# Start addresses of the feed-forward weight forms in a hybrid decoder block

## The chip, the core and the metric

The kernel runs on one core of one Trainium2 chip. The metric is the device time of one execution in microseconds (us), as the median of the runs shown. The profile below is one more execution, taken by the hardware profiler.

## What is computed

The reference is one decoder layer over 512 positions with 1024 channels, in float32. First comes a mixer of two branches (a gated short convolution, and a sparse attention with compressed, selected and windowed keys), merged by gates and projected by `w_o`. The change concerns the second half alone, the feed-forward part:

```python
h = rmsnorm(x, norm2_g[l])
gu = h @ w_ffn_in[l]                       # 1024 -> 2 * 2816
g = causal_dwconv(gu[..., :D_FF], ffn_conv_w[l]) + ffn_conv_b[l]
x = x + (jax.nn.silu(g) * gu[..., D_FF:]) @ w_ffn_out[l]
```

## The kernel before

Every dense product is made of three passes of TensorE in a 4-byte format: both operands are split into a high part and a low part (`split`, lines 151 to 154: ScalarE copies the value to the high part, VectorE subtracts), and hi times hi, hi times lo and lo times hi are added up in PSUM (`dense`, lines 400 to 406: for each k the two products with the high weights, lines 403 and 404, and after them all products with the low weights, line 406). In this document a weight tile is the stationary operand that TensorE loads (LDWEIGHTS), 128 x 128 values at a time, 512 bytes in each partition; the activation is the moving operand that streams past it.

**The feed-forward stage.** It works on two tiles of 128 output channels at a time (`ff_strassen`, line 954): 11 pairs of tiles, each once for the gate half (n = 0) and once for the up half (n = 1) of `w_ffn_in`, 22 form sets in all. Each set is a 2 x 2 x 2 product by Strassen's scheme: seven products of 512 contraction rows (4 k) by 256 positions, so 7 x 4 x 3 = 84 matmuls of 128 x 256, 1848 in the whole stage. The activation forms `xf_h` and `xf_l` (lines 795 and 796) are made once and stay: 4 x 7 slices of 256 values, 1024 bytes each. The weight forms are made for each set by `ff_forms` (line 860):

- `a22`, half a weight tile, split into `th` and `tl` (tags `th` and `tl`, two buffers each, lines 871 and 872). The low part is made by ScalarE (minus the value) and a DMA from POOL's queue that adds the weight from memory (`dma_split`, line 156).
- `a11` and `a12`, a whole weight tile, split in the same way into `wh_s` and `wl_s`, buffers of the ring that the down projection also uses (`ring`, line 162).
- Two pairs of sums of the four blocks, forms 2 and 3 and forms 4 and 1, built by VectorE in `sf` buffers and split by ScalarE and VectorE into `sh` and `sl` (`put`, lines 880 to 885, 44 calls; tags `sh` and `sl`, three buffers each, NSQ = 3).

`ff_pair` (line 904) multiplies: first `a22` (`th`, `tl`), then `a11` and `a12` (`wh_s`, `wl_s`), then forms 2, 3, 4 and 1 (`sh`, `sl`). ScalarE copies the first finished product out of PSUM into `p1` (line 941), and VectorE's `sums` (line 919) adds it to the next bank. Between the two sets of a pair, `down_part` (line 975) does a part of the down projection with matmuls of 128 x 512 (`pdn`; moving `ah`/`al`, weights `wh_d`/`wl_d`). The framework's scheduler orders the instructions on each engine by a timeline of its own and puts in the waits.

**Where buffers start.** A pool hands out its buffers one behind the other, in the order in which the tags first appear, so a tile that is made only to claim a place (a `const` by the name of `gap`, or a first tile with a name that ends in `_`) moves what comes behind it. The pool `pw` (line 797) is such a row. What matters below is the start of a buffer behind a multiple of 512 bytes, here called its **place**. A weight slice is 512 bytes and a slice of `xf` 1024, so the place is the same for all k and all forms of a buffer. In this program the places are:

| buffers | place (bytes) | distance from `xf` |
|---|---|---|
| `xf_h`, `xf_l` | 288 | 0 |
| `th`, `tl` (two each) | 288 | 0 |
| `sh`, `sl` (three each) | 480 | 192 |
| `wh_s`, `wl_s`, `wh_d`, `wl_d` | 480 | 192 |
| `ah`, `al` (moving in the down projection) | 480 | 192 |

In the parts of the program ahead of the feed-forward stage nearly every moving and stationary tile is at place 480, so their distance is 0. The scores of the attention (lines 596 and 597) are the exception: the keys `kHH` and `kL` have rows of 544 values, and the distance between the queries (weights) and the keys (moving) is 0, 128, 256 or 384 by group, branch and first column.

Of the kernel before, what the change touches and what calls it, by code (L numbers as in the profile page):

```python
# [11 lines left out]
F32 = mybir.dt.float32  # L12
F32R = mybir.dt.float32r
# [5 lines left out]
P = 128  # L19
D = 1024  # L20
# [35 lines left out]
NSQ = 3  # L56
# [26 lines left out]
def tile_block(ctx: ExitStack, tc: tile.TileContext, xT, pos, par, par2, w_tok, w_a3, w_gate, w_ao, w_bo, w_o,  # L83
# [11 lines left out]
    def const(shape, name, dt=F32, pool=sb):  # L95
        return pool.tile(shape, dt, name=name, tag=name)

    def w_tmp(name, shape):

        t = pp.tile([P, TOKC], F32, name=name, tag="w4", bufs=NW4)  # L100
        v = t[:, :math.prod(shape)]
        if len(shape) == 2:
            v = v.rearrange("p (a b) -> p a b", a=shape[0])
        elif len(shape) == 3:
            v = v.rearrange("p (a b c) -> p a b c", a=shape[0], b=shape[1])
        return v
# [7 lines left out]
    def s_bank(name):  # L114
        return bank("s", name, 3)

    def t_bank(name):
        return bank("t", name, 2)

    def o_bank(name):  # L120
        return bank("o", name, 1)
# [29 lines left out]
    def split(h, l, v):  # L151
        hi = nc.scalar.activation(h, v, AF.Copy)  # L152
        nc.vector.tensor_sub(l, v, h.bitcast(F32))  # L153
        return hi

    def dma_split(h, l, raw, src, dst=None):

        nc.scalar.activation(h, raw, AF.Copy)  # L158
        nc.scalar.activation(l, raw, AF.Copy, scale=-1.0)  # L159
        nc.gpsimd.dma_start(l if dst is None else dst, src, accum_op=ALU.add)  # L160

    def ring(name):
        return (wf.tile([P, D], F32R, name=f"wh_{name}", tag="wh", bufs=NWF),
                wf.tile([P, D], F32R, name=f"wl_{name}", tag="wl", bufs=NWF))

    def raw_tile(name):
        return wf.tile([P, D], F32, name=f"wr_{name}", tag="wr", bufs=NRAW)
# [202 lines left out]
    def row_scales(total, name, bank_of, dg):  # L370

        pr = bank_of(f"pr_{name}")
        for t in range(NT):
            for i, v in enumerate(total):
                sums = nc.tensor.matmul(pr[:, 2 * t:2 * t + 2], v[:, t * P:(t + 1) * P], ones[:, 0:2],
                                        start=i == 0, stop=i == len(total) - 1)
        ms = sb.tile([P, NT], F32, name=f"ms_{name}", tag="ms")
        nc.vector.tensor_scalar(ms, pr[:, 0:2 * NT].rearrange("p (t two) -> p t two", two=2)[:, :, 0], 1.0 / D, EPS,
                                op0=ALU.mult, op1=ALU.add)
        means[name] = ms  # L380
        r = sb.tile([P, NT], F32, name=f"r_{name}", tag=f"r_{name}")
        rsqrt(r, ms, NT)
        nc.vector.tensor_tensor(dg, ident[:, None, :].to_broadcast([P, NT, P]), r[:, :, None].to_broadcast([P, NT, P]),
                                op=ALU.mult)
        for t in range(NT):
            rows = nc.tensor.matmul(pr[:, t * P:(t + 1) * P], ones, dg[:, t, :], start=True, stop=True)
        rb = sb.tile([P, S], F32, name=f"rb_{name}", tag="rb")
        nc.scalar.activation(rb, pr, AF.Copy)
        return r, rb, (sums, rows)

    r1, r1b, _ = row_scales((sq_sum[0][:, 0],), "n1", d_bank, w_tmp("dg_n1", (NT, P)))
# [8 lines left out]
    def dense(acc, units, first=True, last=True):  # L400

        for i, (wh, wl, xh, xl) in enumerate(units):
            nc.tensor.matmul(acc, wh, xh, start=first and i == 0, stop=False)  # L403
            nc.tensor.matmul(acc, wh, xl, start=False, stop=False)  # L404
        for i, (wh, wl, xh, xl) in enumerate(units):
            nc.tensor.matmul(acc, wl, xh, start=False, stop=last and i == len(units) - 1)  # L406
# [381 lines left out]
    TH = S // 2  # L788
# [6 lines left out]
    xf_h = const([P, 4, 7, TH], "xf_h", F32R, px)  # L795
    xf_l = const([P, 4, 7, TH], "xf_l", F32R, px)
    pw = ctx.enter_context(tc.tile_pool(name="pw", bufs=1, side="left"))
    for i in "hl":
        pw.tile([P, D // 2], F32R, name=f"t{i}_", tag=f"t{i}", bufs=2)
    const([P, 48], "gap_w", F32, pw)  # L800

    def x_forms(k, v):
        nc.vector.tensor_sub(v[:, T1:T3 + 1], v[:, 1:4:2], v[:, 0:2])
# [56 lines left out]
    def ff_forms(f, n):  # L860

        nm = f"{n}_{f}"
        raws = []
        for m in range(2):
            raw = raw_tile(f"s{nm}{m}")
            nc.sync.dma_start(raw, w_ff[f + m, n])
            raws.append(raw)
        a11, a12 = raws[0][:, 0:HALF_D], raws[0][:, HALF_D:]
        a21, a22 = raws[1][:, 0:HALF_D], raws[1][:, HALF_D:]
        form = {}  # L870
        h = pw.tile([P, HALF_D], F32R, name=f"th{nm}", tag="th", bufs=2)
        l = pw.tile([P, HALF_D], F32R, name=f"tl{nm}", tag="tl", bufs=2)
        dma_split(h, l, a22, w_ff[f + 1, n][:, HALF_D:])
        form["a22"] = (h, l)
        h, l = ring(f"s{nm}")
        dma_split(h, l, raws[0], w_ff[f, n])
        form["a11"] = (h[:, 0:HALF_D], l[:, 0:HALF_D])
        form["a12"] = (h[:, HALF_D:], l[:, HALF_D:])

        def put(i, j, v):  # L880
            h = pw.tile([P, D], F32R, name=f"sh{i}{j}{nm}", tag="sh", bufs=NSQ)
            l = pw.tile([P, D], F32R, name=f"sl{i}{j}{nm}", tag="sl", bufs=NSQ)
            split(h, l, v)
            form[i] = (h[:, 0:HALF_D], l[:, 0:HALF_D])
            form[j] = (h[:, HALF_D:], l[:, HALF_D:])

        s = {}

        def pair(i, j):
            v = pw.tile([P, D], F32, name=f"s{i}{j}{nm}", tag="sf", bufs=NSF)  # L890
            s[i], s[j] = v[:, 0:HALF_D], v[:, HALF_D:]
            return v

        v = pair(2, 3)
        nc.vector.tensor_sub(s[3], a11, a21)
        nc.vector.tensor_sub(s[2], a22, s[3])
        put(2, 3, v)
        v = pair(4, 1)
        nc.vector.tensor_sub(s[4], a12, s[2])
        nc.vector.tensor_add(s[1], a21, a22)  # L900
        put(4, 1, v)
        return form

    def ff_pair(f, n, c, form, late=None):
        nm = f"{n}_{f}"
        b1, b26 = o_bank(f"p1{nm}"), t_bank(f"p26{nm}")
        b45, b37 = s_bank(f"p45{nm}"), s_bank(f"p37{nm}")
        lo, hi = slice(0, TH), slice(TH, S)

        def units(wf_, x, ks):  # L910
            wh, wl = form[wf_]
            return [(wh[:, k * P:(k + 1) * P], wl[:, k * P:(k + 1) * P], xf_h[:, k, x], xf_l[:, k, x]) for k in ks]

        def product(acc, wf_, x):
            dense(acc, units(wf_, x, range(4)))

        def sums(dst, bank, v):

            nc.vector.tensor_tensor(dst, bank.rearrange("p (a t) -> p a t", a=2), v[:, None, :].to_broadcast([P, 2, TH]),
                                    op=ALU.add)  # L920

        p1 = pw.tile([P, TH], F32, name=f"p1{nm}", tag="p1", bufs=2)
        c1, c2 = c[:, :, 0:TH], c[:, :, TH:]
        plan = [(b26, hi, 2, T2, True), (b37, hi, 3, T3, True), (b37, lo, 4, B22, False), (b45, hi, 1, T1, True),
                (b1, lo, "a11", B11, True), (b26, lo, "a12", B21, False), (b45, lo, "a22", T4, False)]
        if late is not None:

            for b, cols, wf_, x, opens in plan:
                for i, (wh, wl, xh, xl) in enumerate(units(wf_, x, range(3))):
                    for lhs, rhs, st in ((wh, xh, True), (wh, xl, False), (wl, xh, False)):  # L930
                        nc.tensor.matmul(b[:, cols], lhs, rhs, start=opens and st and i == 0, stop=False,
                                         skip_group_check=True)

            def product(acc, wf_, x):
                (wh, wl, xh, xl), = units(wf_, x, (3,))
                for lhs, rhs, last in ((wh, xh, False), (wh, xl, False), (wl, xh, True)):
                    nc.tensor.matmul(acc, lhs, rhs, start=False, stop=last, skip_group_check=True)

        product(b45[:, lo], "a22", T4)
        product(b1[:, lo], "a11", B11)  # L940
        nc.scalar.activation(p1, b1[:, lo], AF.Copy)
        product(b26[:, lo], "a12", B21)
        product(b26[:, hi], 2, T2)
        sums(c1, b26, p1)
        product(b37[:, hi], 3, T3)
        product(b37[:, lo], 4, B22)
        sums(c2, b37, c1[:, 1])
        product(b45[:, hi], 1, T1)
        sums(c[:, 1].rearrange("p (a t) -> p a t", a=2), b45, c2[:, 1])
        nc.vector.tensor_add(c2[:, 0], c2[:, 0], b45[:, hi])  # L950
# [121 lines left out]
```

## Time and profile before

| | |
|---|---|
| median of 3 runs | 720.97 us (720.72, 720.97 and 1447.38) |
| the profiled execution | 719.79 us, its span 718.1 us |
| TensorE, matmuls | 711.1 us busy, 4309 matmuls |
| TensorE, weight loads | 635.5 us busy |
| VectorE, ScalarE, GpSimd | 532.5, 437.7 and 183.3 us busy |
| the stage from 480 to 690 us | 210 us with 1510 matmuls |
| granted TensorE clock | 1.0 in all 40 slices |

The span runs from the first instruction of the core to the last. A matmul's end is modelled and matmuls overlap, so its length in the profile (277 ns for 128 x 256) is not what it costs; its cost is the time from its start to the next matmul's start, called its **step** here, and for a run of matmuls the difference of two starts by their number. In a row of the timeline the first number is the start in us from the span's start, the second the length, then engine, line, operation, out<-in (moving operand first), shape and count; rows of one kind that follow each other are merged (x4).

### The profile page before, as it was taken

The numbers are of one execution on the slowest core, as the hardware profiler recorded it, in microseconds if no ns is written. First come the engines' busy times: TensorE is split into PE (matmuls) and PEld (weight loads), VectorE is DVE, ScalarE is ACT, GpSimd is POOL, SyncE is SP. The second block draws the span as 40 slices with busy tenths as digits, with TensorE's granted clock in tenths as the row PEclk, the third lists the DMA queues.
The fourth block names the chain that finished last, engine by engine and source line by source line (L and its number), as shares of the span: only waits on it lengthen the run. The fifth ranks groups of instructions, "written<-read, shape, count | busy, mean of one in ns | idle before, by whom it ended". The sixth has DMA issues, their size and how long they took to land.

```text
span 718.1 us, 11433 instructions
## 1 busy us (share of the span) xinstructions
PE 711.1 (99%) x4309; PEld 635.5 (89%) x4309; DVE 532.5 (74%) x973; ACT 437.7 (61%) x738; POOL 183.3 (26%) x176
## 2 busy tenths in 40 slices
PE   9999999999999999999999999999999999999997
PEld 8999888888888888887889999899999999999986
DVE  6887885677568676465695899997787877878643
ACT  7535655877667767443585776676564766646430
POOL 3151422133433333435011211221211222111110
PEclk9999999999999999999999999999999999999999
DMA  7333677511111221062676798987878778785575
GB/s 272 98 94 118 177 175 175 120 60 58 60 60 60 77 70 60 1 234 70 223 191 135 164 230 210 226 202 186 201 187 220 172 184 202 187 205 104 120 140 151
DMA packets 41143, 105.48 MB, mean 147 GB/s; under 512 B 3968, under 2 KB 9216, under 8 KB 41088
## 3 DMA queue, kind: packets, MB, share of 16 engines
q1 hardware_dynamic: 26528, 70.41, 29.8%
q0 software_dynamic: 14272, 34.08, 27.4%
q8 instruction: 34, 0.56, 0.3%
q10 hardware_dynamic: 288, 0.26, 0.1%
q14 instruction: 21, 0.17, 0.1%
HBM read 102.64 MB, written 2.10 MB: 146 GB/s over the span
## 4 chain that ended last, share of the span: by engine, by line
PE 96%; POOL 1%; DVE 1%; ACT 1%; DMA 1%; issue 0%; ACTq 0%
PE p L404 9%; PE p L406 9%; PE p L403 9%; PE pdn L404 6%; PE pdn L403 6%; PE pdn L406 6%; PE pg L403 4%; PE pg L404 4%; PE pg L406 4%; PE pa L403 3%; PE pa L406 3%; PE pa L404 3%; PE pt L650 2%; PE po L406 2%; PE po L403 2%; PE po L404 2%
## 5 line engine op out<-in xcount | busy, mean ns | idle before, releaser
L404 PE MATMUL p<-xf_l,sh 128*128 128x256 f32 x336 | 80.6, 277 | 0.0
L403 PE MATMUL p<-xf_h,sh 128*128 128x256 f32 x336 | 80.6, 277 | 0.0
L152 ACT ACTIVATE sh<-s 128x1024 fp32r<-128x1024 f32 x44 | 46.2, 1057 | 38.2 <-PE p L404 24.5
L404 PE MATMUL pdn<-al,wh_d 128*128 128x512 f32 x176 | 68.8, 391 | 0.0
L403 PE MATMUL pdn<-ah,wh_d 128*128 128x512 f32 x176 | 68.6, 391 | 0.0
L404 PEld LDWEIGHTS p<-xf_l,sh 128*128 128x128 f32 x336 | 63.0, 188 | 0.1
L403 PEld LDWEIGHTS p<-xf_h,sh 128*128 128x128 f32 x336 | 63.0, 188 | 0.1
L160 POOL DMA_DIRECT2D wl_s<-in_w_ff_dram x22 | 19.5, 885 | 167.6 <-ACT wl_s L159 156.1
L153 DVE TENSOR_TENSOR sl<-s,sh 128x1024 fp32r<-128x1024 f32 x44 | 53.8, 1225 | 8.7 <-ACT sh L152 8.7
L158 ACT ACTIVATE wh_s<-wr_s 128x1024 fp32r<-128x1024 f32 x22 | 23.3, 1057 | 53.5 <-PE pdn L404 50.1
L135 POOL TENSOR_TENSOR wl_g<-wr_g,wh_g 128x1024 fp32r<-128x1024 f32 x16 | 38.4, 2402 | 64.4 <-ACT wh_g L133 31.1
L406 PE MATMUL p<-xf_h,sl 128*128 128x256 f32 x336 | 51.6, 277 | 0.0
L403 PE MATMUL pg<-xg_h,wh_g 128*128 128x512 f32 x128 | 51.0, 398 | 0.0
L404 PE MATMUL pg<-xg_l,wh_g 128*128 128x512 f32 x128 | 50.7, 396 | 0.0
L406 PE MATMUL pdn<-ah,wl_d 128*128 128x512 f32 x176 | 47.7, 389 | 0.0
L160 POOL DMA_DIRECT2D wl_d<-in_w_dn_dram x22 | 26.5, 1203 | 77.6 <-ACT wl_d L159 70.4
L991 DVE TENSOR_TENSOR x<-x,pdn 128x512 f32<-128x512 f32 x48 | 33.1, 690 | 16.2 <-PE pdn L406 15.5
L406 PEld LDWEIGHTS p<-xf_h,sl 128*128 128x128 f32 x336 | 44.5, 188 | 0.2
L403 PE MATMUL p<-xf_h,wh_s 128*128 128x256 f32 x168 | 40.5, 277 | 0.0
L404 PE MATMUL p<-xf_l,wh_s 128*128 128x256 f32 x168 | 40.5, 277 | 0.0
L406 PEld LDWEIGHTS pdn<-ah,wl_d 128*128 128x128 f32 x176 | 33.0, 188 | 6.8
L404 PEld LDWEIGHTS pdn<-al,wh_d 128*128 128x128 f32 x176 | 33.1, 188 | 6.2
(348 smaller groups left out, 2138.4 us busy)
## 6 DMA issues: line engine op xcount, KB each, us to landing
wr_s<-in_w_ff_dram SPq DMA_DIRECT2D x44, 512.0 KB, 5.1
wl_s<-in_w_ff_dram POOLq DMA_DIRECT2D x22, 512.0 KB, 7.6
wr_d<-in_w_dn_dram SPq DMA_DIRECT2D x22, 512.0 KB, 6.5
wl_d<-in_w_dn_dram POOLq DMA_DIRECT2D x22, 512.0 KB, 8.5
wr_g<-in_w_gate_dram SPq DMA_DIRECT2D x16, 512.0 KB, 3.4
wr_a<-in_w_a_dram SPq DMA_DIRECT2D x12, 512.0 KB, 4.2
tl<-in_w_ff_dram POOLq DMA_DIRECT2D x22, 256.0 KB, 7.3
wl_a<-in_w_a_dram POOLq DMA_DIRECT2D x10, 512.0 KB, 7.5
```

What stands on the lines that cost most here:

```text
L135: e.tensor_sub(lo[:, 0:n], raw[:, 0:n], hi[:, 0:n].bitcast(F32))
L152: hi = nc.scalar.activation(h, v, AF.Copy)
L153: nc.vector.tensor_sub(l, v, h.bitcast(F32))
L158: nc.scalar.activation(h, raw, AF.Copy)
L160: nc.gpsimd.dma_start(l if dst is None else dst, src, accum_op=ALU.add)
L403: nc.tensor.matmul(acc, wh, xh, start=first and i == 0, stop=False)
L404: nc.tensor.matmul(acc, wh, xl, start=False, stop=False)
L406: nc.tensor.matmul(acc, wl, xh, start=False, stop=last and i == len(units) - 1)
L650: nc.tensor.transpose(pt[:, i * P:(i + 1) * P], e[:, i, kt * P:(kt + 1) * P], ident)
L991: nc.vector.tensor_add(xj, xj, acc)
```

## The change

Three things are done in the pool `pw` and nothing else is touched. `sh` and `sl` become six tags of one buffer each (`sh0`, `sh1`, `sh2`, `sl0`, `sl1`, `sl2`), claimed first, each followed by a gap of 64 bytes; the calls of `put` take them in turn, beginning with number 1. `th` is claimed behind them, with a gap of 64 bytes between it and `tl`. And `p1`, for whose second buffer there is no room any more, has one buffer in place of two.

```diff
-    for i in "hl":
-        pw.tile([P, D // 2], F32R, name=f"t{i}_", tag=f"t{i}", bufs=2)
-    const([P, 48], "gap_w", F32, pw)
+
+    n_sum = []
+
+    def sum_tile(c, i, name):
+        return pw.tile([P, D], F32R, name=name, tag=f"s{c}{i}", bufs=1)
+
+    for c in "hl":
+        for i in range(NSQ):
+            sum_tile(c, i, f"s{c}{i}_")
+            const([P, 16], f"gap_{c}{i}", F32, pw)
+    pw.tile([P, D // 2], F32R, name="th_", tag="th", bufs=2)
+    const([P, 16], "gap_t", F32, pw)
...
         def put(i, j, v):
-            h = pw.tile([P, D], F32R, name=f"sh{i}{j}{nm}", tag="sh", bufs=NSQ)
-            l = pw.tile([P, D], F32R, name=f"sl{i}{j}{nm}", tag="sl", bufs=NSQ)
+            n_sum.append(nm)
+            h, l = (sum_tile(c, len(n_sum) % NSQ, f"s{c}{len(n_sum) % NSQ}x{i}{j}{nm}") for c in "hl")
             split(h, l, v)
...
-        p1 = pw.tile([P, TH], F32, name=f"p1{nm}", tag="p1", bufs=2)
+        p1 = pw.tile([P, TH], F32, name=f"p1{nm}", tag="p1", bufs=1)
```

The places of the changed program, and how many matmuls use each as weights (an `sh` buffer serves 16 in each call of `put`, an `sl` buffer 8; the 44 calls fall 14, 15 and 15 times on numbers 0, 1 and 2):

| buffer | place | distance from `xf` | before | matmuls |
|---|---|---|---|---|
| `sh0` | 288 | 0 | 192 | 224 |
| `sh1` | 352 | 64 | 192 | 240 |
| `sh2` | 416 | 128 | 192 | 240 |
| `sl0` | 480 | 192 | 192 | 112 |
| `sl1` | 32 | 256 | 192 | 120 |
| `sl2` | 96 | 320 | 192 | 120 |
| `th` | 160 | 384 | 0 | 176 |
| `tl` | 224 | 448 | 0 | 88 |
| `wh_s`, `wl_s` | 480 | 192 | 192 | 528 |

`sf` and `p1` move from place 480 to place 224. Every other buffer of the program keeps its address. All five engines and the queues have the same instructions in the same order as before; of the waits, only some of ScalarE's differ, since `p1` has one buffer (line 941 then waits for VectorE or for an instruction of its own engine beside TensorE).

## The prediction

> **What bounds the kernel now.** I began with the page: which engine is busy, and whose work ends last.
>
> ```profile
> PE 711.1 (99%) x4309; PEld 635.5 (89%) x4309; DVE 532.5 (74%) x973; ACT 437.7 (61%) x738; POOL 183.3 (26%) x176
> ...
> PE 96%; POOL 1%; DVE 1%; ACT 1%; DMA 1%; issue 0%; ACTq 0%
> ```
>
> TensorE is busy for 99% of the span, and it makes up 96% of the chain that ended last. So the time is a count of matmuls times their steps, and what VectorE, ScalarE or a DMA gains or loses shows only if TensorE comes to wait for it. Next the busy time by stretch, for the feed-forward stage once it runs evenly:
>
> ```profile
> 480.00:690.00 210.00, 210.00 (x1510) 196.74 (x1509) 161.36 (x225) 123.15 (x162) 39.83 (x40) 1.00 0.77 178
> ```
>
> The columns are the length, then TensorE, weight loads, VectorE, ScalarE and GpSimd. TensorE is busy for all 210 us, at a full clock. VectorE has 161 us to do in 210, ScalarE 123. Nothing in this stage waits in front of TensorE, so only the steps of the matmuls themselves can change. The groups by line say whether they are alike:
>
> ```profile
> L404 PE MATMUL p<-xf_l,sh 128*128 128x256 f32 x336 | 80.6, 277 | 0.0
> L404 PE MATMUL p<-xf_l,wh_s 128*128 128x256 f32 x168 | 40.5, 277 | 0.0
> L404 PE MATMUL p<-xf_l,th 128*128 128x256 f32 x84 | 21.1, 282 | 0.0
> L406 PE MATMUL p<-xf_h,sl 128*128 128x256 f32 x336 | 51.6, 277 | 0.0
> L406 PE MATMUL p<-xf_h,tl 128*128 128x256 f32 x84 | 13.7, 283 | 0.0
> ```
>
> They are not. Work of one shape takes 277 ns with `sh`, `sl` and `wh_s`, and 282 and 283 with `th` and `tl`, and those two are the weights that lie at the same place as `xf`. The timeline gives the steps, here for two products of twelve matmuls at a point where no down projection has run yet:
>
> ```profile
> 410.94 0.28 PE L403 MATMUL p<-xf_h,th 128*128 128x256 f32 x1
> 411.05 0.28 PE L404 MATMUL p<-xf_l,th 128*128 128x256 f32 x1
> ...
> 411.89 0.64 PE L406 MATMUL p<-xf_h,tl 128*128 128x256 f32 x4
> ...
> 412.38 0.28 PE L403 MATMUL p<-xf_h,wh_s 128*128 128x256 f32 x1
> ...
> 413.74 0.28 PE L403 MATMUL p<-xf_h,wh_s 128*128 128x256 f32 x1
> ```
>
> The product with `th` and `tl` lasts from 410.94 to 412.38, 1.44 us or 120 ns a step; that with `wh_s` and `wl_s` to 413.74, 1.36 us or 113.3 ns. Distance 0 costs 6.7 ns a step more than distance 192. But distance 192 isn't always fast:
>
> ```profile
> 425.62 0.39 PE L403 MATMUL pdn<-ah,wh_d 128*128 128x512 f32 x1
> 425.85 0.28 PE L403 MATMUL p<-xf_h,sh 128*128 128x256 f32 x1
> ...
> 428.56 1.10 PE L406 MATMUL p<-xf_h,sl 128*128 128x256 f32 x8
> 429.51 0.28 PE L403 MATMUL p<-xf_h,sh 128*128 128x256 f32 x1
> ```
>
> Here 23 matmuls with `sh` take 2.71 us, 117.8 ns a step, and 8 with `sl` 0.95 us, 118.7: the same buffers, the same distance, 4.5 ns slower. The stretch begins behind a few matmuls of the down projection. I call this the long rhythm and 113.3 ns the short one; it holds from 380 to 400.4 us, around 428, and from 441 to 480.8. The matmuls of the stage in these stretches:
>
> ```profile
> 380.00:400.40 20.40, 18.44 (x153) 1.00 0.62 116
> 425.80:430.50 4.70, 4.65 (x40) 1.00 0.97 283
> 441.00:480.80 39.80, 21.90 (x177) 1.00 0.92 215
> ```
>
> Together 370, of them some 320 with weights at distance 192: 320 x 4.5 ns = 1.4 us. From 480.8 us on the short rhythm holds, and each pair there begins with `th` and `tl`.
>
> **The change, part by part.** No instruction is added, removed or moved, so there is no work to cost; what is left are the steps, the buffer of `p1`, and the speed of the engines that write the forms.
>
> *`th` and `tl` leave distance 0.* 264 matmuls. Their mean over the stage is a little below 120, since the first ones of a run come in faster: 282 or 283 against 277 ns is 5 to 6. I take 5.9. At best the gain is 264 x 5.9 = 1.6 us.
>
> *`sh0` comes to distance 0.* 224 matmuls, by the same row 224 x 5.9 = 1.3 us lost. These two nearly cancel. It hangs on the other six distances, 64, 128, 256, 320, 384 and 448, and on the state. The stage shows none of them. The nearest rows are the attention's scores, matmuls of 128 x 256 too, at distance 128 (the first pair) and 0 (the second):
>
> ```profile
> 216.31 0.28 PE L596 MATMUL sc<-kHH,qT 128*128 128x256 f32 x1
> 216.42 0.28 PE L597 MATMUL sc<-kL,qT 128*128 128x256 f32 x1
> 216.54 0.39 PE L404 MATMUL pg<-xg_l,wh_g 128*128 128x512 f32 x1
> ...
> 242.72 0.28 PE L596 MATMUL sc<-kHH,qT 128*128 128x256 f32 x1
> 242.83 0.28 PE L597 MATMUL sc<-kL,qT 128*128 128x256 f32 x1
> 242.95 0.39 PE L661 MATMUL po<-pl,v_t 128*128 128x512 f32 x1
> ```
>
> Two steps take 0.23 us at either distance, 115 ns a step, between the short rhythm and distance 0. So 128 is no better than 0 here, though two matmuls are a short run. If 128 is like 0 while 192 is not, the pattern has a period of 128 bytes, and 192 is fast because it lies 64 off.
>
> By that reading distances 0, 128, 256 and 384 cost what `th` costs now, and 64, 192, 320 and 448 what `sh` costs now. Dear are then `sh0` 224, `sh2` 240, `sl1` 120 and `th` 176, 760 matmuls where 264 are dear today: 496 more, x 5.9 ns = **+2.9 us**. From this comes off what the long rhythm loses less: runs at a dear distance stand before the short rhythm in the rows (410.94 to 412.38, and the starts of all pairs from 480.8 on), and there would be more of them. I take half of 1.4 us, **-0.7 us**. Together +2.2 us.
>
> The bounds for a step. From above 120 ns, the dearest that the stage shows: all 1848 at 120 would be 1848 x 6.7 = 12.4 us less the 1.6 and 1.4 lost today, +9.4 us. From below what the streaming alone takes, by shapes of 384 and 512 columns:
>
> ```profile
> 41.69 0.33 PE L254 MATMUL pj_s<-wh_t,xg_l 128*128 128x384 f32 x1
> ...
> 42.91 0.33 PE L255 MATMUL pj_o<-wl_t,xg_h 128*128 128x384 f32 x1
> ...
> 690.01 0.39 PE L404 MATMUL pdn<-al,wh_d 128*128 128x512 f32 x1
> ...
> 691.37 0.39 PE L404 MATMUL pdn<-al,wh_d 128*128 128x512 f32 x1
> ```
>
> Seven steps in 1.22 us are 174 ns for 384 columns, six in 1.36 us 227 ns for 512: 128 columns cost 53 ns, 256 then 105. A gap with no overhead left would be 8 ns under the short rhythm, for the 1320 matmuls that move 10.6 us, with the 1.6 and 1.4 us -13.6 us. No row of 256 columns comes near that, so I keep it as an outer bound only.
>
> *`p1` with one buffer.* ScalarE's copy now waits until VectorE has read the last one:
>
> ```profile
> 547.75 0.69 DVE L919 TENSOR_TENSOR c<-p,p 128x512 f32<-128x512 f32 x1 [2.11 <-PE p L406]
> ...
> 560.68 0.36 ACT L941 ACTIVATE p<-p 128x256 f32<-128x256 f32 x1
> ...
> 563.16 0.69 DVE L919 TENSOR_TENSOR up<-p,p 128x512 f32<-128x512 f32 x1 [1.99 <-PE p L406]
> ```
>
> The read of the set before ended at 548.44, the next copy starts at 560.68: 12 us of cover, so the wait costs nothing. Were it gone, the copy would hold up ScalarE's splits behind it and then the products that need them.
>
> *Engines that write the forms.* A slower or faster split would stay hidden in VectorE's 49 us and ScalarE's 87 us of spare time in 210, unless it grew by about a third. I take nothing for it.
>
> **The sum.** The profiled execution took 719.79 us around its span of 718.1; +2.2 makes 722.0. The median of the runs lies 1.18 us above that execution, so I forecast **723.2 us**.
>
> **The rivals.**
>
> *Place doesn't matter at all* (as far as TensorE goes). Then `th` and `tl` must be slow for another reason, for instance because they come first behind the down projection. Against it stand the rows at 410.94, where no down projection had run, and `tl`, the last four of its product, at 283 ns. For it: the long rhythm shows that equal places can cost different times. Near to it is a period of 512 bytes in which only distance 0 is dear: -1.6 + 1.3 = -0.3 us. Time 720.97 us by the one, 720.7 by the other.
>
> The Trainium skill speaks for this rival: by "SBUF — State Buffer", section "Who interferes with whom", TensorE reads the moving operand and the weights through two independent ports and never waits for anyone. By that page the change would be worth nothing, 720.97 us. The rows of `th` against `sh`, 5 to 6 ns apart, don't agree with it as they stand.
>
> *The short rhythm is lost.* It may be the dear `th` and `tl` at the head of each pair that bring TensorE from the down projection back into the short rhythm; behind the down projection without them, at 425.85, the long rhythm came. Put `th` at a harmless distance, and what follows could run at 117.8 ns for the whole stage. The place is the hand-over at each pair, the price 4.5 ns for each of the 1088 matmuls at cheap distances, 4.9 us less the 1.4 us lost today, with the 2.9 us for the dear ones +6.4 us: 727.4 us. It decides once more than half of the stage is slow. Against it: `sh0` or other dear runs may do the same service a few products later.
>
> *Faster.* Distance 0 is the only dear one and its short runs matter less, or the mixed distances end the long rhythm: -1.6 us for `th` and `tl`, -1.4 us for the long-rhythm stretches, and `sh0` at worst +1.3 of it back. With `sh0` harmless in runs of 8 it is -3.0 us: 718.0 us. For it speaks that the first steps behind a switch are not yet at 120 (410.94 to 411.05 is 0.11). It turns the sign as soon as fewer than about 260 matmuls run dear.
>
> **How the numbers follow.** The forecast, a period of 128 bytes: 0.36. Place doesn't matter: 0.12; distance 0 alone is dear: 0.15. Fast state lost: 0.17. Faster: 0.18. Something outside these, by the outer bounds: 0.02. The range for 8 in 10 takes in the first two whole and most of the others: 717.5 to 728.5 us; the forecast's own range, with the step at 5 to 6.7 ns and the long-rhythm stretches kept or ended, is 722 to 724.5. A change of 2% is 14.4 us, about what a measurement of this kernel can tell from no change; none of the cases reaches it and the outer bounds, -13.6 and +9.4 us, stay below it. Faster by over 2%: 0.02, within 2%: 0.95, slower: 0.03.
>
> **What would show it right or wrong.** In the profile of the changed kernel the groups of `th`, `sh0`, `sh2` and `sl1` should read 281 to 283 ns, those of `tl`, `sh1`, `sl0`, `sl2` and `wh_s` 276 to 278; TensorE should stay busy throughout from 480 us on. If `sh2`, `sl1` and `th` read 277, the period is not 128. If all read alike, place doesn't matter; if `wh_s` reads 281 over the whole stage, the short rhythm is lost. If TensorE idles in the stage, the argument is wrong at its root.

## The result, and the profile after

| | before | after |
|---|---|---|
| median of 3 runs | 720.97 us | 725.02 us (724.99 to 725.27) |
| the profiled execution | 719.79 us, span 718.1 | 725.02 us, span 723.3 |

The changed kernel takes 1.0051 [1.0032, 1.0071] times as long as the one before: half a per cent, 4.1 us between the medians and 5.2 us between the two spans. The 1447.38 us among the runs before is one slow run that nothing here explains, and the ratio is of fast runs alone. It is the span that the traces can explain.

The busy time of the engines and the chain that ended last, of the changed kernel:

```profile
PE 716.8 (99%) x4309; PEld 640.8 (89%) x4309; DVE 533.1 (74%) x973; ACT 438.2 (61%) x738; POOL 182.1 (25%) x176
...
PE 96%; POOL 1%; DVE 1%; ACT 1%; DMA 1%; issue 0%; ACTq 0%
```

The same 4309 matmuls, 5.7 us more of TensorE; VectorE and ScalarE moved by half a microsecond, and TensorE is still 96% of the chain. Then the stretch of the feed-forward stage:

```profile
480.00:690.00 210.00, 210.00 (x1483) 197.01 (x1482) 159.58 (x221) 122.93 (x161) 38.97 (x40) 1.00 0.76 175
```

TensorE is busy for all 210 us at the full clock, as before, but it gets through 1483 matmuls where it got through 1510. Nothing waits; each matmul takes longer. Which ones, the groups by line say (each group is one line of `dense`, so an `sh` buffer shows half of its matmuls; one of the 22 sets, the first, is issued from other lines, which leaves 112 here for the buffers numbered 1 and 2 where all the sets have 120):

```profile
L404 PE MATMUL p<-xf_l,wh_s 128*128 128x256 f32 x168 | 41.5, 279 | 0.0
L404 PE MATMUL p<-xf_l,sh0x 128*128 128x256 f32 x112 | 27.9, 283 | 0.0
L404 PE MATMUL p<-xf_l,sh2x 128*128 128x256 f32 x112 | 27.8, 281 | 0.0
L404 PE MATMUL p<-xf_l,sh1x 128*128 128x256 f32 x112 | 27.1, 279 | 0.0
L404 PE MATMUL p<-xf_l,th 128*128 128x256 f32 x84 | 21.1, 284 | 0.0
L406 PE MATMUL p<-xf_h,sl1x 128*128 128x256 f32 x112 | 17.8, 282 | 0.0
L406 PE MATMUL p<-xf_h,sl2x 128*128 128x256 f32 x112 | 17.6, 279 | 0.0
L406 PE MATMUL p<-xf_h,sl0x 128*128 128x256 f32 x112 | 17.0, 277 | 0.0
L406 PE MATMUL p<-xf_h,tl 128*128 128x256 f32 x84 | 13.4, 279 | 0.0
```

There are now three levels where there were two. At 281 to 284 ns stand `sh0`, `sh2`, `sl1` and `th`, the four at distances 0, 128, 256 and 384. At 277 stands `sl0` alone. And at 279 stands the rest, at distances 64, 192, 320 and 448, and among them `wh_s`, whose buffers didn't move: 277 before, 279 now. Such a mean can be a mixture: of the two runs of `sh1` in the set that begins at 498.17 us, the first eight matmuls take 113.5 ns a step (502.42 to 503.33) and the second eight 117.9 (503.81 to 504.75). The starts tell the levels apart. The timeline, from the head of a set (in this stretch the down projection runs ahead of every set, not only between the two of a pair):

```profile
498.17 0.28 PE L403 MATMUL p<-xf_h,th 128*128 128x256 f32 x1
...
499.13 0.63 PE L406 MATMUL p<-xf_h,tl 128*128 128x256 f32 x4
499.60 0.28 PE L403 MATMUL p<-xf_h,wh_s 128*128 128x256 f32 x1
...
501.01 0.28 PE L403 MATMUL p<-xf_h,wh_s 128*128 128x256 f32 x1
```

Eight matmuls with `th` in 0.96 us are 120 ns a step; four with `tl` in 0.47 and twelve with `wh_s` and `wl_s` in 1.41 us are 117.5. That is the long rhythm, in a stretch where the kernel before had the short one (there the same twelve took 1.36 us). The end of a set, in the same view:

```profile
489.88 0.28 PE L403 MATMUL p<-xf_h,sh0x 128*128 128x256 f32 x1
...
490.84 0.62 PE L406 MATMUL p<-xf_h,sl0x 128*128 128x256 f32 x4
491.30 0.28 PE L403 MATMUL p<-xf_h,sh0x 128*128 128x256 f32 x1
...
492.26 0.62 PE L406 MATMUL p<-xf_h,sl0x 128*128 128x256 f32 x4
492.71 0.39 PE L403 MATMUL pdn<-ah,wh_d 128*128 128x512 f32 x1
```

`sh0` at distance 0 takes 0.96 us for eight, 120 ns a step, and right behind it the last four, `sl0` at distance 192, take 0.45 us, 113 ns. So behind a run at distance 0 the short rhythm is back. Behind `th`, which now lies at 384 and is just as dear, it isn't.

The mean step over the whole stage, from the differences of the starts. In each kernel three steps of 200 ns and more, all before 391 us, are left out, so 1845 of the 1848 matmuls stand here; sums of the steps of this stage further down leave out such steps too. The kernel before has no numbered sums, so its column gives the mean of all `sh` or all `sl`:

| buffer (distance after) | matmuls | before, ns | after, ns | lost, us |
|---|---|---|---|---|
| `sh0` (0) | 224 | 114.3 | 119.7 | 1.2 |
| `sh2` (128) | 240 | 114.3 | 118.0 | 0.9 |
| `sl1` (256) | 120 | 114.4 | 119.5 | 0.6 |
| `th` (384) | 176 | 118.7 | 118.9 | 0.0 |
| `tl` (448) | 88 | 120.0 | 117.7 | -0.2 |
| `wh_s`, `wl_s` (192) | 527 | 114.1 | 117.6 | 1.8 |
| `sh1` (64) | 238 | 114.3 | 115.8 | 0.4 |
| `sl2` (320) | 120 | 114.4 | 117.0 | 0.3 |
| `sl0` (192) | 112 | 114.4 | 114.0 | 0.0 |

Together 212.1 us before and 217.1 us after: 5.0 of the 5.2 us by which the span grew. A little over half, 2.7 us, stands at the dear distances, and 2.5 us at cheap ones in the long rhythm; `tl` takes off 0.2.

### The profile page after: what moved, and what is told of

It is laid out like the page before. It is cut to its first block, busy times and chain, and to the rows that moved or that the text cites. A ratio compares the mean times of both kernels' runs of the same rounds, so it can differ in the third digit from the quotient of the medians.

```text
span 723.3 us, 11449 instructions
## 1 busy us (share of the span) xinstructions
PE 716.8 (99%) x4309; PEld 640.8 (89%) x4309; DVE 533.1 (74%) x973; ACT 438.2 (61%) x738; POOL 182.1 (25%) x176
## 4 chain that ended last, share of the span: by engine, by line
PE 96%; POOL 1%; DVE 1%; ACT 1%; DMA 1%; issue 0%; ACTq 0%
PE p L404 10%; PE p L403 10%; PE p L406 10%; PE pdn L404 6%; PE pdn L403 6%; PE pdn L406 6%; PE pg L403 4%; PE pg L404 4%; PE pg L406 4%; PE pa L406 3%; PE pa L403 3%; PE pa L404 3%; PE pt L650 2%; PE po L406 2%; PE po L403 2%; PE po L404 2%
## 5 line engine op out<-in xcount | busy, mean ns | idle before, releaser
L403 PEld LDWEIGHTS pdn<-ah,wh_d 128*128 128x128 f32 x176 | 33.0, 188 | 6.2
L654 DVE TENSOR_TENSOR pl<-pt,ph 128x512 fp32r<-128x512 f32 x40 | 27.0, 683 | 15.1 <-ACT ph L653 15.0
L403 PE MATMUL pa<-xg_h,wh_a 128*128 128x512 f32 x96 | 37.9, 395 | 0.0
L627 ACT ACTIVATE e<-e,sums 128x512 f32<-128x512 f32 (+3 forms) x64 | 30.9, 554 | 11.5 <-DVE sums L601 9.0
L623 ACT ACTIVATE e<-sc,mx 128x256 f32<-128x256 f32 (+3 forms) x64 | 33.1, 521 | 7.6 <-DVE mx L622 7.5
L404 PE MATMUL pa<-xg_l,wh_a 128*128 128x512 f32 x96 | 37.7, 393 | 0.0
L406 PE MATMUL pg<-xg_h,wl_g 128*128 128x512 f32 x128 | 34.7, 394 | 0.0
L403 PEld LDWEIGHTS p<-xf_h,wh_s 128*128 128x128 f32 x168 | 31.5, 188 | 0.1
```

The lines of the kernel that those rows point to most:

```text
L623: nc.scalar.activation(e[:, i, 0:nk], sc[:, o:o + nk], AF.Exp, bias=mx[:, i], accum_out=sums[:, i])
L627: nc.scalar.activation(v, v, AF.Copy, scale=sums[:, i])
L654: nc.vector.tensor_sub(pl, pt, ph.bitcast(F32))
```

## The experiments

The theory has two parts. *Distance:* with 256 columns a weight tile at a multiple of 128 bytes from the moving operand is dear. *Rhythm:* the down projection leaves TensorE in the long rhythm, and a run at distance 0, which `th` and `tl` were before at the head of each set, brings the short one back. The texts written ahead of the runs call this A. Its main rival, B, has the loss in the mix of six places among the sums, with no part in it for `th` and `tl`. Other rivals are named where they come in. Each kernel has the same instructions in the same order as the two above; only starts of buffers, and in some the buffers of `p1`, differ. Each was timed in five rounds beside the kernel before.

### `th` and `tl` put back

The changed kernel, with `th` and `tl` at distance 0 again and all else as changed.

```diff
+    for i in "hl":
+        pw.tile([P, D // 2], F32R, name=f"t{i}_", tag=f"t{i}", bufs=2)
     for c in "hl":
         for i in range(NSQ):
             sum_tile(c, i, f"s{c}{i}_")
             const([P, 16], f"gap_{c}{i}", F32, pw)
-    pw.tile([P, D // 2], F32R, name="th_", tag="th", bufs=2)
-    const([P, 16], "gap_t", F32, pw)
```

> The changed kernel with th and tl back at place 288 (distance 0 from xf); the six sum buffers keep the places of the change, p1 keeps one buffer. Theory A (a weight place costs by its distance modulo 128: at a multiple of 128 about 119.5 ns a step; at 64 off, 113.3 or 117.7 ns, and which of the two is set by the runs that stood before): th and tl at distance 0 hand the short rhythm on to wh_s and wl_s, so these 528 matmuls fall from 117.6 to 113.3 ns (-2.2 us), tl rises from 117.7 to 120 (+0.2 us): about 723.0 us, the groups of wh_s and wl_s at 277 ns instead of 279. Theory B (the 117.6 ns of wh_s come from the mixture of places in the stage, not from what stands before them): nothing changes for wh_s, 725.0 to 725.3 us.

Measured: 723.62 us, 1.0051 [1.0036, 1.0066] times the kernel before in the same rounds (720.58); span 721.7, 1.6 us less than the changed kernel's. Its groups:

```profile
L404 PE MATMUL p<-xf_l,wh_s 128*128 128x256 f32 x168 | 40.4, 276 | 0.0
L404 PE MATMUL p<-xf_l,sh0x 128*128 128x256 f32 x112 | 28.0, 283 | 0.0
...
L406 PE MATMUL p<-xf_h,tl 128*128 128x256 f32 x84 | 13.7, 283 | 0.0
```

`wh_s` is back at 276 (from 480 us on its mean step is 113.3 ns), though neither it nor `xf` was touched, and `tl` is dear again. The sums keep their levels. So `th` and `tl` decide what the matmuls behind them cost, and B falls. The ratios of this kernel and of the change lie too close for their intervals; the spans and the groups tell the two apart.

### `th` and `tl` moved, the sums left

The kernel before, with `th` at distance 384 and `tl` at 448 and the sums at 192 as they were: the other half of the change alone.

```diff
-    for i in "hl":
-        pw.tile([P, D // 2], F32R, name=f"t{i}_", tag=f"t{i}", bufs=2)
     const([P, 48], "gap_w", F32, pw)
+    for i in "hl":
+        pw.tile([P, D], F32R, name=f"s{i}_", tag=f"s{i}", bufs=NSQ)
+    const([P, 48], "gap_a", F32, pw)
+    pw.tile([P, D // 2], F32R, name="th_", tag="th", bufs=2)
+    const([P, 16], "gap_b", F32, pw)
...
-        p1 = pw.tile([P, TH], F32, name=f"p1{nm}", tag="p1", bufs=2)
+        p1 = pw.tile([P, TH], F32, name=f"p1{nm}", tag="p1", bufs=1)
```

> The kernel before with th at place 160 and tl at 224 (distances 384 and 448, as in the change), all sum buffers at 480 as before, p1 with one buffer. Theory A: with no dear run ahead of them that ends at distance 0, wh_s, wl_s and all sums stay at 117.7 ns: 1584 matmuls x (117.7 - 114.25) = +5.4 us, tl 0.2 us cheaper: about 726.2 us, the groups of sh, sl, wh_s, wl_s at 280 to 281 ns. Theory B (each place has a cost of its own, whatever stands before): th as dear as before, tl 88 x 6 ns cheaper, -0.5 us: about 720.4 us, sh and sl at 277 ns.

Measured: 725.71 us, 1.007 [1.0057, 1.0083]; span 724.4. The groups:

```profile
L404 PE MATMUL p<-xf_l,sh 128*128 128x256 f32 x336 | 82.5, 279 | 0.0
...
L404 PE MATMUL p<-xf_l,wh_s 128*128 128x256 f32 x168 | 41.5, 279 | 0.0
...
L404 PE MATMUL p<-xf_l,th 128*128 128x256 f32 x84 | 21.1, 283 | 0.0
```

The weights of 264 matmuls were moved, and the other 1584, which weren't, went from 277 to 279: a mean step of 117.6 to 117.9 for all of them, all through the stage. Alone this half costs about as much as the whole change: the steps of the stage add up to 217.1 us in both, and the two intervals overlap. In the whole change the dear sums cost more than the long rhythm would, but behind `sh0` and at the step from `wl_s` to `sh1` the short rhythm comes back for parts of a set.

### The six sums at distance 128, and at 64

The kernel before, with all six buffers of `sh` and `sl` at one place, 416 (distance 128) in the one kernel and 352 (distance 64) in the other.

```diff
-    const([P, 48], "gap_w", F32, pw)
+    const([P, 32], "gap_w", F32, pw)      # 16 for distance 64
+    for i in "hl":
+        pw.tile([P, D], F32R, name=f"s{i}_", tag=f"s{i}", bufs=NSQ)
+    const([P, 16], "gap_f", F32, pw)      # 32 for distance 64
```

> The kernel before with all sh and sl buffers at place 416 (distance 128 from xf), th, tl, wh_s and wl_s and p1 as before. Theory A (period of 128 bytes): sh and sl are as dear as th, 118 to 119.5 ns for 1056 matmuls that take 114.3 now: +3.9 to +5.5 us, 725 to 726.5 us, their groups at 281 to 283 ns. Theory C (period of 512 bytes, only distance 0 is dear): 720.97 us and 277 ns.

> The kernel before with all sh and sl buffers at place 352 (distance 64 from xf), the rest as before. Theory A: 64 is cheap, and wl_s (distance 192) hands the short rhythm on: 113.3 ns once the stage runs evenly, 720.3 to 721.6 us, groups at 276 to 278 ns. Theory B (each distance has a cost of its own; sh1 at 64 takes 115.8 ns in the changed kernel): 1056 x 1.5 ns = +1.6 us, 722.6 us, groups at 279 ns.

Measured: at 128 725.28 us, 1.0068 [1.0056, 1.008], span 723.4; at 64 720.39 us, 0.9995 [0.9987, 1.0004], span 718.5. The groups at 128:

```profile
L404 PE MATMUL p<-xf_l,sh 128*128 128x256 f32 x336 | 83.2, 281 | 0.0
...
L406 PE MATMUL p<-xf_h,sl 128*128 128x256 f32 x336 | 53.2, 282 | 0.2 <-DVE sl L153 0.2
...
L404 PE MATMUL p<-xf_l,wh_s 128*128 128x256 f32 x168 | 40.5, 276 | 0.0
```

and at 64:

```profile
L404 PE MATMUL p<-xf_l,sh 128*128 128x256 f32 x336 | 80.2, 276 | 0.0
...
L406 PE MATMUL p<-xf_h,sl 128*128 128x256 f32 x336 | 51.5, 277 | 0.1
```

Nothing differs between these two programs but 64 bytes in where six buffers start, and they are 4.9 us apart in time and 4.8 in span. `wh_s` is at 276 in the first, so the short rhythm holds up to the sums; `sh` and `sl` alone are dearer, 118.4 and 119.0 ns a step against 113.6 and 113.9. Against the short rhythm, 128 off is dear and 64 off is not. But 118.4 is only 0.7 ns above the long rhythm, so the mean alone doesn't tell a dear distance from a lost rhythm. The single steps do: from 480 us on those of the sums at 128 scatter from 112 to 124 ns, while in a kernel below that runs in the long rhythm throughout (`th` and `tl` at 480) all those of the sums lie between 117 and 119. For 256 and 384 the evidence is `sl1` and `th` in the kernels with these places, at 119.5 and about 119 ns.

### `tl` alone at a cheap distance, then both

In the first kernel `th` stays at distance 0 and only `tl` goes behind the gap, to 192. A rival had it that the last run ahead of `wh_s` must be a dear one for the short rhythm to come. In the second both go to 192, so that no weights of the 256-wide products are at a multiple of 128; if there is no handing on, this should be the shortest of all.

```diff
-    for i in "hl":
-        pw.tile([P, D // 2], F32R, name=f"t{i}_", tag=f"t{i}", bufs=2)
+    pw.tile([P, D // 2], F32R, name="th_", tag="th", bufs=2)
     const([P, 48], "gap_w", F32, pw)
+    pw.tile([P, D // 2], F32R, name="tl_", tag="tl", bufs=2)
```

```diff
+    const([P, 48], "gap_w", F32, pw)
     for i in "hl":
         pw.tile([P, D // 2], F32R, name=f"t{i}_", tag=f"t{i}", bufs=2)
-    const([P, 48], "gap_w", F32, pw)
```

> The kernel before with tl at place 480 (distance 192) and th left at 288 (distance 0); all else as before. Theory A (cost by the distance modulo 128, rhythm handed on from the run before): eight dear matmuls with th, then tl in the short rhythm like the rest: 88 x 6.7 ns = -0.6 us, about 720.0 us, the group of tl at 276 to 277 ns. Rival F (the rhythm needs the whole dear product of twelve): it is lost behind th, tl and 1584 others stay at 117.7 ns: +5.5 us, about 726 us, groups at 279 to 281 ns.

> The kernel before with th and tl both at place 480: every weight of the stage at distance 192, no dear run at all in it. Theory A: nothing brings the short rhythm behind the down projection, all 1848 matmuls take 117.7 ns: 217.5 instead of 212.1 us, +5.4 us, about 726 us, all groups at 279 to 281 ns. Rival E (it is the change of place from th to tl in the changed kernel that spoils the rhythm, not the missing dear run): with one place for all, 113.3 ns throughout, 209.4 us, -2.7 us, about 717.9 us, groups at 276 to 277 ns.

Measured: `tl` alone 719.94 us, 0.9987 [0.9973, 1.0001], span 718.4; both 725.79 us, 1.0066 [1.0047, 1.0085], span 723.5. The groups with `tl` alone moved:

```profile
L404 PE MATMUL p<-xf_l,wh_s 128*128 128x256 f32 x168 | 40.4, 276 | 0.0
...
L406 PE MATMUL p<-xf_h,tl 128*128 128x256 f32 x84 | 13.1, 276 | 0.0
```

and with both:

```profile
L404 PE MATMUL p<-xf_l,sh 128*128 128x256 f32 x336 | 82.6, 279 | 0.0
...
L404 PE MATMUL p<-xf_l,wh_s 128*128 128x256 f32 x168 | 41.5, 279 | 0.0
...
L404 PE MATMUL p<-xf_l,th 128*128 128x256 f32 x84 | 20.9, 280 | 0.0
```

Eight matmuls at distance 0 behind the down projection are enough: `tl` follows them at 276 and saves its 0.5 us. Five are not: in the kernel before, at 467.21 us, one `th` and four `tl` stand alone behind the down projection, and `wh_s` follows them at 117.8 ns a step. Take the eight away as well, so that by distance every matmul is cheap, and the steps of the stage add up to 217.3 us against 211.5, from 480 us on at 117.7 to 118.1 ns in every group. The dear run costs about 5 ns for each of 176 matmuls, 0.9 us, and without it 5.8 us are lost in steps, and as much between the medians. (The spans are 5.1 us apart: with `tl` alone moved TensorE has two longer steps at 416 us that cost it 0.5 us.) A kernel with no dear weights is among the longest measured here.

### A switch between two cheap distances

`th`, `tl`, `wh_s` and `wl_s` all at distance 192, and the sums at 64.

```diff
+    const([P, 16], "gap_s", F32, pw)
+    for i in "hl":
+        pw.tile([P, D], F32R, name=f"s{i}_", tag=f"s{i}", bufs=NSQ)
+    const([P, 32], "gap_t", F32, pw)
     for i in "hl":
         pw.tile([P, D // 2], F32R, name=f"t{i}_", tag=f"t{i}", bufs=2)
-    const([P, 48], "gap_w", F32, pw)
```

> No dear run at all (th, tl, wh_s, wl_s at distance 192), as in the run with th and tl at 480, but all sum buffers at place 352 (distance 64). In the changed kernel a run at 64 that follows a run at 192 in the long rhythm goes at 113.3 ns. Theory A with that (a switch from 192 to 64 also turns the long rhythm into the short one): 792 matmuls at 117.7, 1056 at 113.3 ns, 212.9 us, +0.8 us, about 721.3 us; sh and sl at 276 to 277 ns, wh_s at 279 to 280. If only a dear run turns the rhythm: all at 117.7 ns, 725.8 us, sh and sl at 279 to 281 ns.

Measured: 721.45 us, 1.0016 [1.0007, 1.0024]; span 719.7. The groups:

```profile
L404 PE MATMUL p<-xf_l,sh 128*128 128x256 f32 x336 | 80.4, 277 | 0.0
...
L404 PE MATMUL p<-xf_l,wh_s 128*128 128x256 f32 x168 | 41.3, 279 | 0.0
```

The first 36 of the 84 matmuls of a set run in the long rhythm (117.6 to 118.1 ns from 480 us on), and from the first `sh` on the short one holds (113.4). So distance 0 isn't the only thing that brings it back: the step from weights at 192 to weights at 64 does it too. The changed kernel has the same step, from `wl_s` to `sh1`, and there too the first `sh1` runs at 113 ns. From `tl` at 448 to `wh_s` at 192 it doesn't come.

### Six places, all cheap

B once more, from the other side: six different places among the sums, as in the change, but only distances 64, 192, 320 and 448; `th` at 0, `tl` at 192, `p1` with one buffer. Against the changed kernel:

```diff
+    pw.tile([P, D // 2], F32R, name="th_", tag="th", bufs=2)
     for c in "hl":
         for i in range(NSQ):
+            const([P, 16 if c + str(i) == "h0" else 32], f"gap_{c}{i}", F32, pw)
             sum_tile(c, i, f"s{c}{i}_")
-            const([P, 16], f"gap_{c}{i}", F32, pw)
-    pw.tile([P, D // 2], F32R, name="th_", tag="th", bufs=2)
-    const([P, 16], "gap_t", F32, pw)
+    pw.tile([P, D // 2], F32R, name="tl_", tag="tl", bufs=2)
```

> The sum buffers spread as in the change, one place each, but over the four cheap distances alone: sh0 at 352 (64), sh1 480 (192), sh2 96 (320), sl0 224 (448), sl1 352 (64), sl2 480 (192); th at 288 (distance 0), tl at 480 (192), p1 with one buffer. Theory A (what counts is the distance modulo 128 and the rhythm, not that places differ): no dear run but th, the short rhythm handed on through most of the stage: 719.5 to 721.5 us, all groups but th at 276 to 278 ns. Theory B (mixing places is itself the cost): as slow as the change, 723.5 to 725 us.

Measured: 719.50 us, 0.9987 [0.9978, 0.9996]; span 717.1. The groups:

```profile
L404 PE MATMUL p<-xf_l,sh2x 128*128 128x256 f32 x112 | 26.9, 277 | 0.0
...
L404 PE MATMUL p<-xf_l,sh0x 128*128 128x256 f32 x112 | 26.7, 276 | 0.0
...
L404 PE MATMUL p<-xf_l,th 128*128 128x256 f32 x84 | 21.1, 282 | 0.0
...
L406 PE MATMUL p<-xf_h,sl0x 128*128 128x256 f32 x112 | 17.0, 276 | 0.0
```

Spreading the places costs nothing where the distances are cheap. This is the only kernel of the study whose interval lies below 1: 0.13% under the kernel before. Its steps add up to 1.3 us less, of which `tl` has 0.5; with the steps of 200 ns and more, of which it has five and the kernel before three, 0.8 us are left, near the 1.0 between the spans.

The same with the sums at one place (distance 64), `th` at 0, `tl` at 192 and `p1` with two buffers was to do as well:

```diff
-    for i in "hl":
-        pw.tile([P, D // 2], F32R, name=f"t{i}_", tag=f"t{i}", bufs=2)
-    const([P, 48], "gap_w", F32, pw)
+    pw.tile([P, D // 2], F32R, name="th_", tag="th", bufs=2)
+    const([P, 16], "gap_s", F32, pw)
+    for i in "hl":
+        pw.tile([P, D], F32R, name=f"s{i}_", tag=f"s{i}", bufs=NSQ)
+    const([P, 32], "gap_t", F32, pw)
+    pw.tile([P, D // 2], F32R, name="tl_", tag="tl", bufs=2)
```

> th at 288 (distance 0), tl at 480 (192), all sums at 352 (64), p1 with two buffers. By theory A the two small gains add: tl 0.6 us, sums at 64 behind wl_s 0.2 to 0.9 us (they left the long rhythm sooner when tried alone): 719.2 to 720.2 us, the fastest so far; all groups but th at 276 to 277 ns. If the hand-over fails with this order, groups at 279 to 281 ns and 722 us or more.

Measured: 720.02 us, 0.9992 [0.9983, 1.0001], span 717.3. By the median inside what was expected; its interval holds 1, so it is not told apart from the kernel before.

### `p1` with one buffer

```diff
-        p1 = pw.tile([P, TH], F32, name=f"p1{nm}", tag="p1", bufs=2)
+        p1 = pw.tile([P, TH], F32, name=f"p1{nm}", tag="p1", bufs=1)
```

> The kernel before with one buffer for p1 in place of two, every weight buffer at its old place. The prediction costed this at nothing, since 12 us lie between the last read and the next write: 720.2 to 721.0 us, TensorE without idle time from 480 us on. If the wait costs something, it shows as idle time of ScalarE in front of line 941 and later of TensorE in front of sh: 721.5 us or more.

Measured: 720.16 us, 0.9996 [0.9987, 1.0005], span 718.4. The stretch from 480 us:

```profile
480.00:690.00 210.00, 210.00 (x1510) 196.75 (x1509) 161.61 (x224) 122.69 (x162) 39.84 (x40) 1.00 0.77 178
```

The same 1510 matmuls in the same 210 us as before. The buffer is worth nothing.

### Two that missed: the 512-wide matmuls

If multiples of 128 are dear, the rest of the kernel, which has nearly all its 512-wide matmuls at distance 0, should gain from 64 bytes too. Two kernels tried that: one moves `ah` and `al` to place 32, 64 off the weights of the down projection; the other moves the activations `xg_h` and `xg_l` of the first half to 416, 64 off the weights there.

```diff
-PAD_U = 60
+PAD_U = 52
...
+    const([P, 16], "gap_a", F32, pf)      # ahead of ah and al
```

```diff
-    for name in ("mx1", "mx0", "sums1"):
+    for name in ("mx1", "mx0"):
...
+    pa.tile([P, HG, 1], F32, name="sums1_", tag="sums1", bufs=2)      # behind xg_l
```

> The kernel before with the moving tiles ah and al of the down projection at place 32 instead of 480 (distance 448 from their weights, 64 off a multiple of 128, where it was 0); the conv buffers move with them, all else as before. If the 128-byte rule holds for 512 columns too (theory A widened): 528 matmuls lose the 6.7 ns, 227 to 220 ns, -3.5 us, about 717.1 us, the groups of pdn at 383 to 385 ns instead of 390. Rival G (with 512 columns the loads have time to spare and place does not matter): 720.3 to 720.9 us, pdn at 390 ns. The hand-over to th may shift the first steps of each pair by 0.1 us at most.

> The kernel before with the moving (and, in the token rounds, stationary) tiles xg_h and xg_l of the first half of the program at place 416 instead of 480, 64 off their weights where the distance was 0; nothing in the feed-forward stage changes. If the rule holds for 512 and 384 columns: 720 matmuls of 128x512 and 192 of 128x384 lose up to 6.7 ns each, -4 to -6 us where nothing else is waited for, 715 to 717 us; pg, pa and pkc at 384 to 390 ns instead of 394 to 398. Rival G (only matmuls as short as the load, 256 columns, feel the place): 720.3 to 720.9 us.

Measured: the down projection at 64, 725.37 us, 1.0059 [1.0041, 1.0076], span 723.6; `xg` at 64, 723.23 us, 1.0038 [1.0022, 1.0054], span 720.9. Both are longer, and by neither the theory nor its rival. First `xg`, the groups of the gate products of the kernel before:

```profile
L403 PE MATMUL pg<-xg_h,wh_g 128*128 128x512 f32 x128 | 51.0, 398 | 0.0
L404 PE MATMUL pg<-xg_l,wh_g 128*128 128x512 f32 x128 | 50.7, 396 | 0.0
...
L406 PE MATMUL pg<-xg_h,wl_g 128*128 128x512 f32 x128 | 34.7, 394 | 0.0
```

and of the kernel with `xg` 64 off:

```profile
L404 PE MATMUL pg<-xg_h,wh_g 128*128 128x512 f32 x128 | 51.5, 402 | 0.0
L405 PE MATMUL pg<-xg_l,wh_g 128*128 128x512 f32 x128 | 51.1, 399 | 0.0
...
L407 PE MATMUL pg<-xg_h,wl_g 128*128 128x512 f32 x128 | 35.2, 398 | 0.0
```

With 512 columns it is the other way round: distance 0 is the cheaper one, by 3 to 4 ns of recorded length. The starts say the same: the median step of the groups of `pg` and `pa` goes from 227 or 228 to 233 or 234 ns, and over all 720 matmuls of `pg`, `pa` and `pkc` the steps add up to 3.1 us more, 4.3 ns each, near the 2.8 by which the span grew. The 384-wide products with `xg` stay at a median of 173 ns: with them 64 bytes change nothing. The feed-forward stage of this kernel keeps its 212.1 us. Then the down projection:

```profile
L404 PE MATMUL p<-xf_l,sh 128*128 128x256 f32 x336 | 82.1, 279 | 0.0
L404 PE MATMUL pdn<-al,wh_d 128*128 128x512 f32 x176 | 68.9, 392 | 0.0
...
L406 PE MATMUL pdn<-ah,wl_d 128*128 128x512 f32 x176 | 48.2, 392 | 0.0
L404 PE MATMUL p<-xf_l,wh_s 128*128 128x256 f32 x168 | 41.2, 278 | 0.0
```

In the kernel before the group of `wl_d` reads

```profile
L406 PE MATMUL pdn<-ah,wl_d 128*128 128x512 f32 x176 | 47.7, 389 | 0.0
```

Here too the 512-wide matmuls gain nothing (`wl_d` 392 against 389 before; the steps of the three groups add up to 0.8 us more), but most of the loss, 4.2 of the 5.5 us between the spans, is in the steps of the 256-wide ones, `sh` and `wh_s`, which weren't touched. The timeline at the head of a set:

```profile
512.65 0.28 PE L403 MATMUL p<-xf_h,th 128*128 128x256 f32 x1
...
513.61 0.64 PE L406 MATMUL p<-xf_h,tl 128*128 128x256 f32 x4
514.09 0.28 PE L403 MATMUL p<-xf_h,wh_s 128*128 128x256 f32 x1
...
515.51 0.28 PE L403 MATMUL p<-xf_h,wh_s 128*128 128x256 f32 x1
```

`th` and `tl` are at distance 0 and take their 120 ns, and yet `wh_s` follows in the long rhythm, 1.42 us for twelve or 118.3 ns. The theory as it stood falls here: a run at distance 0 doesn't always bring the short rhythm back. Eight and more do behind the down projection at distance 0, and twelve don't behind the one at 448 (weights at 480, `ah` and `al` at 32). What is handed on depends on the run before it as well.

## Why the prediction was right, and where it was not

The time lay inside the range, 1.8 us above the forecast and 0.5 us above the likeliest case's own range of 722 to 724.5. The miss is larger than that looks: the forecast of +2.2 us stands against +5.2 in the spans, and the 1.18 us that were added for the way from the profiled execution to the median weren't there after (both 725.02 us). The profiled execution of the kernel before was one of its shortest (719.79 us; 33 later ones have a median of 720.50 and begin at 719.66). That this made up for part of the miss is luck. The remark that 2% is about what a measurement can tell was too wide as well: the interval of 1.0032 to 1.0071 tells half a per cent from nothing. By steps:

- *TensorE alone sets the time, and only the steps can change.* Right: 210 us busy in 210 us after as before, and the steps account for 5.0 of 5.2 us.
- *The period of 128 bytes.* Right, and on thin ground: two rows of the attention's scores were all that spoke for it, two steps each (to the ns 117 and 120 at distance 128, 113 and 119 at 0). The four buffers named as dear are the four at 281 to 284 ns, and the 4.9 us between the sums at 128 and at 64 show for these two that 64 bytes decide. The term of +2.9 us measured +2.7 for the dear four and -0.2 for `tl`, 2.5 together.
- *The long rhythm will be lost less, -0.7 us.* Wrong in sign; this is the step that failed, and it measured +2.5 us. The prediction saw rightly that the run of `th` and `tl` at distance 0 brings TensorE back from the down projection. It inferred that any dear run does so, and that more of them would help. The trace of after has the counter-example: behind `sh0` at distance 0 `sl0` runs at 113 ns, behind `th` at 384 `tl` and `wh_s` run at 117.5, and behind `sl1` at 256 `sh1` at 118. Dear and restoring are not the same thing. The kernel with only `th` and `tl` moved shows it for the whole stage.
- *The rival "the short rhythm is lost"* had the right mechanism and its own price for the worst of it, +6.4 us. It came true for a third of each set (`tl`, `wh_s` and `wl_s`, 28 of 84) and parts of the rest; `sh0` did the service "a few products later" that was named against it. The two cases aren't alternatives, as the chances took them, but two terms of one sum: 2.5 + 2.5 us.
- *"Place doesn't matter".* Refuted. The rule of the Trainium skill that stood for it ("SBUF — State Buffer", "Who interferes with whom") has TensorE reading the moving operand and the weights through independent ports without ever waiting; moving only the six weight buffers of the sums by 64 bytes is worth 4.9 us of 720, so the measurement decides against it for this use. What inside TensorE or the memory makes the period is not shown by any run here.
- *`p1` with one buffer costs nothing.* Right: 0.9996 [0.9987, 1.0005] by itself.
- *The engines that write the forms.* Right as far as the end goes: VectorE's work in the stretch went from 161.4 to 159.6 us and ScalarE's from 123.2 to 122.9, with fewer sets falling into it, and TensorE never waits for either.

Left open: what makes the two rhythms, whether behind `th` at 384 it is that distance or the switch to `tl` at 448 that keeps the long one (no kernel has `th` at 384 with `tl` at 192 behind it), why a switch from 192 to 64 brings the short one and one from 448 to 192 doesn't, and why 512 columns feel a distance of 64 the other way. The runs show that each is so, not why.

## What to carry to other kernels

Where TensorE is busy without a gap, as in this stage, the start of a weight buffer relative to the moving operand can be worth some per cent of a matmul's step (113.3 against 118 to 120 ns here): compare the steps of groups of one shape, from start to start, before looking for waits. A local cost may be what keeps the work behind it cheap, so change one buffer's place at a time, time the whole, and read the groups that were not touched. What holds at 256 columns need not hold at 512: the sign turned.

## What the runs showed that was not expected

- With 256 columns a step takes 113.3 or 117.7 ns at distances 64, 192, 320 and 448, and 118 to 120 at 0, 128, 256 and 384. Which of the two cheap values holds is decided by what ran before, and it can then hold through the rest of a set, 72 matmuls in the kernel before.
- Eight matmuls at distance 0 at the head of a set, 0.04 us dearer, decide over 76 behind them (719.94 against 725.79 us); five at that distance did not bring the short rhythm back.
- With 512 columns distance 0 is the cheaper one: 64 bytes off, the products with `xg` take 4.3 ns a step more (by recorded length 402, 399 and 398 ns against 398, 396 and 394), and the distance of the 512-wide matmuls also decides the rhythm of the 256-wide ones behind them.
